# Pooling by banded products on TensorE, with 24 expert tiles transposed inside the pool mixer from GpSimd's queue

## The chip, the cores and the metric

One core of a Trainium2 chip runs the whole program in one launch. The metric is the device time in microseconds. TensorE (PE) multiplies, PEld is its weight load, VectorE is DVE, ScalarE is ACT, GpSimd is POOL, and SyncE (SP) issues the DMAs of the kernel before, all but its gathers.

## The reference

The input x is 512 tokens of 1024 features, in float32. Two blocks follow each other; the second one's first half and its expert half are given here in words.

```python
# block one, pool_mixer: windows w = 2, 4, 8, 16, a group of 512 channels each
u, z = split(x @ w_in)                              # 2048 columns each
m_g = (csum(u_g) - csum(u_g) lagged w) / min(t + 1, w) - u_g
m   = concat(m_g @ w_grp[g]) * scale
x   = layer_norm(ALPHA * x + (m * silu(z)) @ w_out)
# block two, first half
ada = silu(c) @ w_ada + b_ada                       # six vectors of 1024
# a conv branch and a gated linear recurrence (rg_lru), head norms, w_out
# block two, expert half (peer): top 16 of 128 x 128 experts for 8 heads,
# gelu(expert_u[idx] . h) * softmax(score), summed over expert_v[idx]
```

## The kernel before, in words

Every float32 product is made of three: an operand is split into a float32r part and its remainder (`split`, L108: the copy on ACT, the subtraction on DVE or, where asked, on POOL), and `mm3` (L138) multiplies high by high, high by low and low by high. Weights come through `wload` (L122), which splits them on the way; every `nload[1]`-th of them has its subtraction on POOL.

**The pool mixer** (the front) runs over the four groups. `x_group(g)` builds pooled tokens with the time axis along the free dimension: log2(w) shifted additions of `xT` on DVE, a scaled subtraction, a repair of the first w - 1 tokens, a split. `m_group` multiplies the group's `w_in` columns by that, so pooling comes ahead of the product. `gate_group` multiplies by `w_grp`, then scales by silu(z) (`z_group`); `y_group` multiplies by `w_out` and adds into `ya`. The last group goes through `last_group`, behind `p1.close()`, which gives the memory of the mixer's pools to those of the next stage (`wp2` among them, from which `last_group` takes its weights). In between, `ada(j)` sums 512 columns of `w_ada` on DVE from eight loads, and `ada_fin(j)` finishes them; its split has `pool=True`.

**The recurrence stage** (conv and lru branches) takes 20 products of 512 columns of the second `w_in`, each over eight slices of the features (`zchunk` and `zhalf`), with a chain of DVE and ACT work behind each (`lru`, `conv`, `headnorm`). Every weight's subtraction is on POOL here (`NZ = 1`). Between the products `pre_u` (L542) takes 20 tiles of `expert_u`, 128 rows each: four loads of half a tile into `praw`, one DVE transpose into `put`, one store to `ut_d`, and the same for the second half, all issued by SP, with two buffers of each kind.

**The expert half** finds the top keys, turns the scores into a dense weight matrix and runs over 128 tiles of experts. `stage_a(i)` takes a tile in one of three ways: for `i < NU` from `ut_d`, already transposed; for `NU <= i < RT = 38` by eight TensorE transposes; after that by a DVE transpose of its own load.

The program is traced in source order. A planner then orders each engine's instructions by its own cost model, with the source order as the priority, so that work of a later stage may stand early in a queue: polynomial work of L559 to L575 stands in the front on DVE, for one.

## Time and profile before

| | us |
|---|---|
| three runs, median (lowest to highest) | 1996.67 (1991.03 to 1996.69) |
| profiled execution, own time | 1993.15 |
| its span, first to last instruction | 1991.4 |
| PE busy in the span | 1800.5 |
| DVE busy in the span | 1783.6 |

The profiled execution's time is 1.75 us over its span. The front takes about 350 us of the span and the recurrence stage the next 200; the dense expert loop runs from about 1100 to the end. Busy shares are averages over stages with different limits, so a stage is read by its own window.

### The profile page before, as it was taken

How to read it: one execution, taken by the hardware profiler on the slowest of the kernel's cores; microseconds unless marked ns; L12 is line 12 of the kernel's file. 1: busy time of each engine (PE TensorE's matmuls, PEld its weight loads, DVE VectorE, ACT ScalarE, POOL GpSimd, SP SyncE). 2: the span in 40 equal slices, each digit the busy share in tenths (PEclk: the TensorE clock that was granted, in tenths of full speed). 3: DMA queues.
4: the chain of work that ended last, by engine and by line, in shares of the span. 5: the costliest groups of instructions: out<-in, count | busy, mean ns of one | idle time of the engine just before them, and what ended most of it. 6: DMA issues, size and time to landing. Idle time of an engine off the chain costs nothing.

```text
span 1991.4 us, 26565 instructions
## 1 busy us (share of the span) xinstructions
PE 1800.5 (90%) x9003; PEld 1568.3 (79%) x9003; DVE 1783.6 (90%) x3088; ACT 830.8 (42%) x1318; POOL 727.5 (37%) x492
## 2 busy tenths in 40 slices
PE   8999889896899978888887999998999998989997
PEld 6787677765689978888766898888888887878886
DVE  8989888889868999996897998999999999999956
ACT  4433333444553339988332332333232333332334
POOL 3113222333351000000133655556565556565514
PEclk9999999998899989999998999999999999999999
DMA  5554574465554233545959999999999999999922
GB/s 163 180 166 128 190 250 131 140 203 179 172 159 135 76 112 139 202 179 205 294 199 281 299 285 292 302 296 309 306 298 296 310 299 289 305 293 306 293 102 96
DMA packets 288293, 441.13 MB, mean 222 GB/s; under 512 B 24600, under 2 KB 203652, under 8 KB 285084
## 3 DMA queue, kind: packets, MB, share of 16 engines
q1 hardware_dynamic: 251292, 305.19, 51.1%
q0 software_dynamic: 36864, 134.23, 20.5%
q8 instruction: 71, 1.16, 0.2%
q14 instruction: 66, 0.54, 0.1%
HBM read 393.11 MB, written 46.23 MB: 221 GB/s over the span
## 4 chain that ended last, share of the span: by engine, by line
DVE 36%; DMA 24%; PE 17%; issue 12%; ACT 7%; SPq 2%; POOL 2%; DVEq 0%; POOLq 0%; ACTq 0%
DMA uraw<-in_expert_u 11%; DVE ut L540 5%; DMA gu<-in_expert_u,idx 3%; DMA gv<-in_expert_v,idx 3%; DMA araw<-in_w_ada 3%; PE bank L139 3%; PE bank L141 3%; PE bank L140 3%; ACT gs L1136 2%; DVE acc L1204 2%; DVE ul L117 2%; DVE wlo L117 2%; ACT o L1098 2%; DVE junk L1193 2%; DVE sw L240 2%
## 5 line engine op out<-in xcount | busy, mean ns | idle before, releaser
L115 POOL TENSOR_TENSOR wlo<-wraw,whi 128x1024 fp32r<-128x1024 f32 x111 | 292.3, 2635 | 782.4 <-ACT whi L113 766.8
L141 PE MATMUL aux<-h2h,ul 128*128 128x384 f32 x1024 | 360.7, 353 | 59.8 <-DVE ul L117 53.5
L139 PE MATMUL aux<-h2h,uh 128*128 128x384 f32 x1024 | 355.9, 348 | 4.9 <-ACT uh L884 1.8
L140 PE MATMUL aux<-h2l,uh 128*128 128x384 f32 x1024 | 353.6, 345 | 0.0
L113 ACT ACTIVATE whi<-wraw 128x1024 fp32r<-128x1024 f32 x218 | 228.3, 1051 | 196.4 <-DMA wraw<-in_expert_v 68.5
L140 PE MATMUL o<-wlo,wh 128*128 128x512 f32 x756 | 297.7, 394 | 13.8 <-DVE wlo L117 13.7
L141 PE MATMUL o<-whi,wl 128*128 128x512 f32 x756 | 296.6, 392 | 0.0
L139 PE MATMUL o<-whi,wh 128*128 128x512 f32 x756 | 290.1, 395 | 5.2 <-ACT whi L113 5.2
L141 PEld LDWEIGHTS aux<-h2h,ul 128*128 128x128 f32 x1024 | 198.6, 194 | 76.6 <-DVE ul L117 68.7
L1181 POOL DMA_INDIRECT gv<-in_expert_v,idx x128 | 186.8, 1460 | 186.0 <-DVE acc L1204 150.4
L1181 POOL DMA_INDIRECT gu<-in_expert_u,idx x128 | 167.5, 1309 | 161.3 <-DVE junk L1193 127.7
L139 PEld LDWEIGHTS aux<-h2h,uh 128*128 128x128 f32 x1024 | 198.6, 194 | 10.3 <-ACT gl L905 2.4
L113 ACT ACTIVATE uh<-ut 128x1024 fp32r<-128x1024 f32 x90 | 95.3, 1058 | 262.2 <-PE aux L140 174.5
L540 DVE STREAM_TRANSPOSE ut<-uraw 128x1024 f32<-128x1024 f32 x90 | 200.0, 2222 | 4.7 <-DMA uraw<-in_expert_u 4.7
L140 PEld LDWEIGHTS aux<-h2l,uh 128*128 128x128 f32 x1024 | 197.9, 193 | 3.7
L1193 DVE SCALAR_TENSOR_TENSOR junk<-gu,hrow 128x1024 bf16<-128x1024 f32 x128 | 168.3, 1315 | 19.8 <-DMA gu<-in_expert_u,idx 19.6
L1204 DVE SCALAR_TENSOR_TENSOR acc<-gv,cf,acc 128x1024 f32<-128x1024 f32 x127 | 169.6, 1335 | 17.6 <-DMA gv<-in_expert_v,idx 15.1
L140 PEld LDWEIGHTS o<-wlo,wh 128*128 128x128 f32 x756 | 143.3, 190 | 43.9 <-DVE wlo L117 16.5
L113 ACT ACTIVATE wh<-gl 128x384 fp32r<-128x384 f32 x128 | 66.7, 523 | 253.2 <-PE o L140 234.3
L139 PEld LDWEIGHTS o<-whi,wh 128*128 128x128 f32 x756 | 143.3, 190 | 33.0 <-ACT whi L113 6.1
L141 PEld LDWEIGHTS o<-whi,wl 128*128 128x128 f32 x756 | 143.3, 189 | 30.7
L117 DVE TENSOR_TENSOR wlo<-wraw,whi 128x1024 fp32r<-128x1024 f32 x107 | 150.6, 1409 | 7.2 <-ACT whi L113 7.2
(376 smaller groups left out, 3607.4 us busy)
## 6 DMA issues: line engine op xcount, KB each, us to landing
wraw<-in_expert_v SPq DMA_DIRECT2D x128, 512.0 KB
uraw<-in_expert_u SPq DMA_DIRECT2D x360, 128.0 KB
araw<-in_w_ada SPq DMA_DIRECT2D x96, 256.0 KB
g_d<-gs SPq DMA_DIRECT2D x24, 1024.0 KB
gt<-g_d SPq DMA_DIRECT2D x15, 1536.0 KB
wraw<-in_pool_w_in SPq DMA_DIRECT2D x32, 512.0 KB
wraw<-in_w_in SPq DMA_DIRECT2D x20, 512.0 KB
praw<-in_expert_u SPq DMA_DIRECT2D x160, 64.0 KB
```

Of the source, the lines that this page charges most:

```text
L113: S.activation(hi, src, AF.Copy)
L115: G.tensor_tensor(lo, src, hi.bitcast(F32), op=OP.subtract)
L117: V.tensor_tensor(lo, src, hi.bitcast(F32), op=OP.subtract)
L139: i = PE.matmul(out, lhsT=l[0], rhs=r[0], start=first, stop=False)
L140: PE.matmul(out, lhsT=l[0], rhs=r[1], start=False, stop=False)
L141: PE.matmul(out, lhsT=l[1], rhs=r[0], start=False, stop=last)
L240: V.tensor_tensor(nxt[:, :, step:], cur[:, :, step:], cur[:, :, :T - step], op=OP.add)
L540: V.transpose(out=ut.rearrange("p k (a r) -> p a k r", r=32), in_=raw.rearrange("p a (c k) -> p a k c", k=KD))
L1098: S.activation(o2[:, u], iorow, AF.Abs, bias=sT[:, 1, t0 + u:t0 + u + 1], scale=-1.0)
L1181: G.indirect_dma_start(out=r, out_offset=None, in_=src, in_offset=bass.IndirectOffsetOnAxis(ap=idx[t][:, s:s + 1], axis=0))
L1193: paced(V.scalar_tensor_tensor(junk, r, 1.0, hrow[t], op0=OP.mult, op1=OP.mult, accum_out=cf[t][:, s:s + 1]))
L1204: paced(V.scalar_tensor_tensor(acc[t], r, cf[t][:, s:s + 1], acc[t], op0=OP.mult, op1=OP.add))
```

## The change

- `u_group(g)` multiplies x (as the stationary operand) by the group's `w_in` columns: tokens on the partitions, 96 products of 512 columns as `m_group` had, in four banks at once, and four splits of 128x512.
- `pooled(g, u)` multiplies u by a banded matrix of w ones less w on the diagonal: for each of 4 x 4 blocks two products of 128 columns and one or two of 16 columns at the block's edge. The scale 1/w is folded into the copy from the bank.
- `bands()` builds the four band matrices and their first-tile forms once. `x_group`, `xT` and its four POOL additions go.
- No subtraction is left on POOL in the front or in the recurrence stage (`NZ`, `nload[1] = 3` removed, the `ada_fin` split on DVE).
- `pre_u` takes 24 tiles instead of 20. All are called inside the mixer's loop over groups 0 to 2, eight per group; its loads and stores are issued by POOL, and its `praw` and `put` buffers lie in the mixer's pool. The calls inside the recurrence find nothing left to do.
- The `ada_fin` calls stand after `gate_group` for groups 1 and 2 and after the loop for the last.

```diff
-AF_ = (1, 1, 0, 0)
-NZ = 1
+AF_ = (1, 1, 1)
+NZ = 1 << 30
-NU = 20
+NU = 24
+NP1 = 1
+BW = P + 16
...
-    sp_ = p1.enter_context(tc.tile_pool(name="sp_", bufs=3))
+    up = p1.enter_context(tc.tile_pool(name="up1", bufs=2))
-    xT = xp.tile([P, KD, T], F32, name="xT")
...
-    for q in range(4):
-        G.tensor_tensor(xT[:, 2 * q:2 * q + 2, :], xh[:, q].bitcast(F32), xl[:, q].bitcast(F32), op=OP.add)
...
+    def u_group(g):
+        bs = [bank() for _ in range(NT)]
+        for kk in range(4):
+            w = wload(w_in[kk * 256:(kk + 1) * 256, g * 512:(g + 1) * 512].rearrange("(k p) c -> p k c", p=P), 2)
+            for t in range(NT):
+                s = slice(t * P, (t + 1) * P)
+                for j in range(2):
+                    x = at(xhl, 2 * kk + j)
+                    mm3(bs[t], (x[0][:, s], x[1][:, s]), (w[0][:, j], w[1][:, j]), kk + j == 0, kk == 3 and j == 1)
+        uh = [act.tile([P, 2, T], F32R, name="ah", tag="ah") for _ in range(2)]
+        ul = [act.tile([P, 2, T], F32R, name="al", tag="al") for _ in range(2)]
+        for t in range(NT):
+            split(uh[t // 2][:, t % 2], ul[t // 2][:, t % 2], bs[t])
+        return uh, ul
+
+    def pooled(g, u):
         r = []
+        band, first, rest = band_[g]
         for c in range(4):
-            w = wcols(w_in, g * 512 + c * P, P)
             b = bank()
-            for k in range(KD):
-                mm3(b, (w[0][:, k], w[1][:, k]), at(xg, k), k == 0, k == KD - 1)
+            part = lambda t, i: u[i][t // 2][:, t % 2, c * P:(c + 1) * P]
+            for t in range(NT):
+                m = (band if t else first)[:, :P]
+                o = b[:, t * P:(t + 1) * P]
+                e = o[:, :16]
+                PE.matmul(o, lhsT=part(t, 0), rhs=m, start=True, stop=False)
+                if t == 0:
+                    PE.matmul(e, lhsT=part(t, 0), rhs=rest, start=False, stop=False)
+                else:
+                    PE.matmul(e, lhsT=part(t - 1, 0), rhs=band[:, P:], start=False, stop=False)
+                    PE.matmul(e, lhsT=part(t - 1, 1), rhs=band[:, P:], start=False, stop=False)
+                PE.matmul(o, lhsT=part(t, 1), rhs=m, start=False, stop=True)
...
-            split(h, l, b)
+            S.activation(h, b, AF.Copy, scale=1.0 / WINDOWS[g])
+            V.scalar_tensor_tensor(l, b, 1.0 / WINDOWS[g], h.bitcast(F32), op0=OP.mult, op1=OP.subtract)
...
-        split(hi, lo, acc, True)
+        split(hi, lo, acc)
...
+    def u_load(raw, i, a0, na, q_=nc.sync):
...
+                    u_load(raw, npre, 2 * h, 2, G)
...
+                    G.dma_start(ut_d[npre, :, h], ut.rearrange("p k e -> p (k e)"))
...
-    xg = act_tiles()
-    list(x_group(0, xg))
-    nload[1] = 3
     accs = {}
-    for g in range(4):
-        mhl = m_group(g, xg)
...
+    mhl = pooled(0, u)
+    for g in range(3):
+        pre_u(NP1)
+        u = u_group(g + 1)
+        pre_u(NP1)
+        pre_u(NP1)
         ghl = gate_group(g, mhl, sz)
         if AF_[g] == 1:
             ada_fins()
-        xg = act_tiles()
-        sz = z_group(g + 1, x_group(g + 1, xg))
+        sz = z_group(g + 1)
+        pre_u(NP1)
+        mhl = pooled(g + 1, u)
...
         for _ in y_group(g, ghl):
-            pass
+            pre_u(1)
+    ada_fins()
     p1.close()
```

## Rows read from the trace of the kernel before

**Rows 1.** The span by stage: busy time of each engine in each stretch (in brackets the instructions), the granted TensorE clock as a share of full speed, the mean busy share of the DMA engines, and GB/s.
```profile
0.00:45.00 45.00, 35.41 (x170) 30.48 (x171) 37.62 (x53) 19.53 (x29) 17.73 (x62) 0.98 0.58 176
45.00:200.00 155.00, 153.18 (x656) 122.34 (x655) 149.55 (x200) 60.04 (x98) 36.80 (x13) 0.99 0.50 155
200.00:350.00 150.00, 135.77 (x619) 108.17 (x618) 128.49 (x167) 48.67 (x73) 39.53 (x21) 0.99 0.59 188
350.00:550.00 200.00, 163.61 (x726) 127.38 (x726) 175.92 (x212) 100.59 (x153) 65.63 (x38) 0.91 0.56 172
550.00:620.00 70.00, 69.94 (x421) 64.16 (x420) 45.44 (x61) 35.80 (x61) 31.40 (x29) 1.00 0.55 173
```

**Rows 2.** What TensorE waited for, from 45 to 350 us: total, times, longest.
```profile
PE bank L140 <- DVE wlo L117: 5.2, 3, 2.9
PE bank L140 <- DVE sl L117: 2.7, 2, 2.2
```

**Rows 3.** What TensorE waited for longest from 350 to 550 us, and then what SP's queue waited for there.
```profile
PE aux L620 <- ACT sq L616: 27.4, 5, 9.1
...
SPq L552 <- DVE put L540: 42.9, 30, 4.6
SPq L124 <- POOL wlo L115: 28.5, 6, 15.6
```

**Rows 4.** TensorE's instructions in order of time (start, us, instruction, how many merged): products of 512 columns, of 256 columns, and of 128 columns, these in plain float32.
```profile
24.08 0.39 PE L139 MATMUL bank<-xh,whi 128*128 128x512 f32 x1
24.31 0.40 PE L140 MATMUL bank<-xl,whi 128*128 128x512 f32 x1
...
16.21 0.28 PE L141 MATMUL bank<-xh,wlo 128*128 128x256 f32 x1
16.33 0.28 PE L139 MATMUL bank<-xh,whi 128*128 128x256 f32 x1
...
799.78 2.84 PE L1135 MATMUL bank<-og,o 128*128 128x128 f32 x24
```

**Rows 5.** Groups of DVE instructions from 0 to 335 us: shapes, count, busy time and mean ns of one, idle time before them.
```profile
L240 DVE TENSOR_TENSOR sw<-xT 128x1022 f32<-128x1022 f32 x16 | 23.8, 1487 | 0.0
L240 DVE TENSOR_TENSOR sw<-sw 128x1020 f32<-128x1020 f32 x12 | 16.7, 1394 | 0.0
L240 DVE TENSOR_TENSOR sw<-sw 128x1016 f32<-128x1016 f32 x8 | 12.1, 1509 | 0.0
L240 DVE TENSOR_TENSOR sw<-sw 128x1008 f32<-128x1008 f32 x4 | 4.8, 1190 | 0.0
L244 DVE SCALAR_TENSOR_TENSOR xe<-sw,xT 128x1024 f32<-128x1024 f32 x16 | 23.6, 1477 | 0.2
L117 DVE TENSOR_TENSOR al<-xe,ah 128x1024 fp32r<-128x1024 f32 x16 | 22.7, 1423 | 0.4 <-ACT ah L113 0.4
L117 DVE TENSOR_TENSOR wlo<-wraw,whi 128x1024 fp32r<-128x1024 f32 x39 | 55.7, 1430 | 1.9 <-ACT whi L113 1.9
L117 DVE TENSOR_TENSOR sl<-bank,sh 128x512 fp32r<-128x512 f32 x16 | 10.8, 681 | 4.3 <-ACT sh L113 4.3
```

**Rows 6.** POOL's and DVE's instructions around 110 us in order of time, the POOL row first.
```profile
110.49 2.41 POOL L115 TENSOR_TENSOR wlo<-wraw,whi 128x1024 fp32r<-128x1024 f32 x1 [17.35 <-ACT whi L113]
...
107.94 1.21 DVE L240 TENSOR_TENSOR sw<-sw 128x1020 f32<-128x1020 f32 x1
110.80 3.18 DVE L240 TENSOR_TENSOR sw<-sw 128x1016 f32<-128x1016 f32 x1
```

**Rows 7.** Groups of POOL instructions from 0 to 335 us (the first two) and from 350 to 550 us (the third).
```profile
L115 POOL TENSOR_TENSOR wlo<-wraw,whi 128x1024 fp32r<-128x1024 f32 x17 | 49.2, 2894 | 169.4 <-ACT whi L113 169.4
L115 POOL TENSOR_TENSOR ahl<-acc,ahl 128x512 fp32r<-128x512 f32 x12 | 23.7, 1975 | 62.9 <-DVE acc L343 36.3 <-ACT ahl L113 14.2 <-DMA ada_d<-araw 9.1
...
L115 POOL TENSOR_TENSOR wlo<-wraw,whi 128x1024 fp32r<-128x1024 f32 x25 | 62.3, 2492 | 126.6 <-ACT whi L113 114.6 <-DMA praw<-in_expert_u 11.9
```

**Rows 8.** The transposes of the pre-turned tiles (group of DVE, 350 to 550 us), and SP's issues of their loads (ns min/median/max, first and last start).
```profile
L540 DVE STREAM_TRANSPOSE put<-praw 128x512 f32<-128x512 f32 x40 | 46.2, 1158 | 12.8 <-DMA praw<-in_expert_u 12.7
L535 SPq DMA_DIRECT2D praw<-in_expert_u x160: 354/425/1389, 365.0 to 521.8; - x160
```

**Rows 9.** The only DMAs that POOL issues in this kernel, gathers of 128 rows: groups from 1100 to 1900 us, and four in order of time (in brackets POOL's idle time before).
```profile
L1181 POOL DMA_INDIRECT gv<-in_expert_v,idx x128 | 186.8, 1460 | 186.0 <-DVE acc L1204 150.4 <-DMA uraw<-in_expert_u 12.4 <-issue 6.4
L1181 POOL DMA_INDIRECT gu<-in_expert_u,idx x119 | 157.7, 1325 | 139.9 <-DVE junk L1193 112.6 <-DMA uraw<-in_expert_u 9.2 <-issue 8.1
...
1226.63 1.28 POOL L1181 DMA_INDIRECT gu<-in_expert_u,idx  x1 [0.30 <-issue]
1228.22 0.94 POOL L1181 DMA_INDIRECT gv<-in_expert_v,idx  x1 [0.30 <-issue]
```

**Rows 10.** The first and last start of one line each: the first DVE work of `last_group`, the last addition of `y_group` (ns min/median/max).
```profile
L297 DVE SCALAR_TENSOR_TENSOR sz<-bank,cols,sz x8: 466/476/485, 324.1 to 344.6; 128x256 f32<-128x256 f32 x8
L329 DVE TENSOR_TENSOR ya<-ya,bank x16: 668/674/680, 188.4 to 302.8; 128x512 f32<-128x512 f32 x16
```

**Rows 11.** A tile's two ways in `stage_a`: subtraction from a bank after TensorE transposes (two per tile), and from `ut` (one per tile), then the TensorE transposes themselves.
```profile
L886 DVE TENSOR_TENSOR ul<-aux,uh x36: 630/680/692, 756.1 to 961.4; 128x512 fp32r<-128x512 f32 x36
L895 DVE TENSOR_TENSOR ul<-ut,uh x20: 1199/1214/1226, 587.7 to 724.2; 128x1024 fp32r<-128x1024 f32 x20
L882 PE MATMUL aux<-ident,uraw x144: 270/273/377, 742.5 to 953.7; 128*128 128x128 f32 x144
```

## What the change will do, predicted blind

> **What bounds the kernel now.** I first cut the span by stage [rows 1], since the page's 90% for both PE and DVE is an average. From 45 to 200 us PE is busy 153 of 155 us and DVE 150: the front is bound by PE, with DVE as full behind it. From 200 to 350 us PE falls to 136 of 150 and DVE to 128: neither is full, and the list of PE's waits [rows 2] names splits on DVE, weights' and banks'. From 350 to 550 us, the recurrence stage, PE is busy 164 of 200 at a granted clock of 0.91, while DVE has 176. PE's longest wait there [rows 3] is for the head norms' squares, the end of chains that alternate between DVE and ACT, so a late DVE is what PE pays for. SP's queue waits 42.9 us there for transposes and 28.5 us for subtractions on POOL, with the next weights' loads behind them. From 550 us PE is full again [rows 1], and what follows is not touched but for four tiles. So the change is worth what it gives in two windows: the front, where PE counts, and the recurrence, where DVE counts.
>
> **PE in the front.** `u_group` has the 96 products of 512 columns that `m_group` had, and `z_group`, `gate_group` and `y_group` stay. Two starts in a row stand 0.23 us apart for 512 columns and 0.12 us for 256 [rows 4]. `pooled` adds 60 products per group (3 for the first token tile and 4 for the others, times 4 blocks of channels), 240 in all, 128 of them with 128 columns and 112 with 16. No such product is in the trace. From above, none should cost more than a 256-column one: 240 x 0.12 = 29 us. From below, by columns alone, (0.23 - 0.12) / 256 = 0.00043 us each: 128 x 0.065 + 112 x 0.018 = 10 us. The nearest row in shape is the plain float32 product of 128 columns, 24 in 2.84 us or 0.118 each [rows 4]; but its operands are not float32r, and the float32r ones run faster for the same columns. I take 0.09: 240 x 0.09 = +22 us, all on PE's path where PE is full. The Trainium skill's page "TensorE: Matmul & The Clock Gate", section "Back-to-back issue gap", gives about 81 ns per product at 128 columns in a stream of weight loads and products; by it the sum here would be 19 us instead of 22, and no row here shows it.
>
> **DVE in the front.** Gone are the shifted additions, 23.8 + 16.7 + 12.1 + 4.8 = 57.4 us, the scaled subtractions, 23.6, and the splits of pooled tokens, 22.7 [rows 5]; with small repairs about 112 us. New are 16 splits of u at 0.68 us (11) [rows 5], 48 transposes at 1.158 us (56) [rows 8], the 17 subtractions that POOL had at 1.21 (21), 12 of `ada_fin` at some 0.68 (8) [rows 5 to 7], and some 40 small operations for the bands, at 0.2 us about 7. That is 103 us, so the work hardly changes: -9 us. What changes is the lock: an addition on DVE that takes 1.21 us took 3.18 us beside a POOL subtraction of 2.41 us [rows 6], and the mean of the weights' subtractions on DVE is 1.43 us, not 1.21 [rows 5]. So one product on POOL took up to 2.0 us from DVE, more than the 1.21 us it saved there. Without them the 39 weights' subtractions alone get back 39 x 0.22 = 9 us, and others perhaps as much again. DVE falls from 316 us of the first 350 to about 288.
>
> For PE I count from this: 3 us at the start (9.6 us idle in the first 45, part of it for pooled tokens that are not needed any more), and half of the 14 us idle from 200 to 350, 7 us; bounds 0 and 17. The front is then 22 - 3 - 7 = +12 us.
>
> **POOL's queue.** POOL now issues 24 x 10 = 240 DMAs, of which SP issued 200 at 0.43 us each [rows 8]. The only DMAs of POOL in the trace are gathers of 128 rows: 0.94 us at the least, 1.39 us in the mean of both groups, with 0.30 us to the next [rows 9]. A load here has 64 pieces of 1 KB and a store 128 of 2 KB. Bounds for one: 0.94 + 0.30 = 1.24 and 1.39 + 0.30 = 1.69 us, so 298 to 405 us for all, from about 3 us on, as nothing else is on POOL and the loads depend on nothing. I take the lower end, since most DMAs here describe half as many pieces: done at about 300 us. The cover is the front itself: the buffers lie in the mixer's pool, which `last_group`'s weights take over, and its first DVE work starts at 324 us [rows 10], at 336 with the 12 us above. That needs 1.35 us or less per DMA (with 12 us for the weights' way to that product, (336 - 12) / 240). If it is more, the weights of `last_group` wait, and DVE, in order, stands at transposes whose data is late; behind those are the subtractions that PE waits for.
>
> The DMA engines have room: they are busy 0.50 to 0.59 of the front at 155 to 188 GB/s [rows 1], and 25 MB more (24 tiles of 0.5 MB, in and out) are 72 GB/s over 350 us, which would bring them to some 0.75 to 0.8.
>
> **The recurrence stage.** DVE loses 40 transposes, 46.2 us [rows 8], and gains 25 subtractions at 1.21 us, 30 us, that were POOL's [rows 7]. The lock gives back at most 25 x 2.0 = 49 us [rows 6]; I take two thirds, 33, since a DVE operation with one operand in SBUF need not stop. So 176 - 46 + 30 - 33 = 127 us of the 200. A weight's remainder is also ready in 1.2 instead of 2.5 us [rows 7], and SP's queue has no transposes to wait for [rows 3]. PE's idle time there is 36 us, and the granted clock of 0.91 says that the engine, after its gaps, spent 18% of the window at 1.2 instead of 2.4 GHz. I take three quarters of the idle time, -27 us; the rest are the chains' own lengths on ACT. Bounds: -8 (the waits on POOL and on praw stay hidden behind the chains) and -45 (all of the idle time and a part of the clock).
>
> **Four tiles** go from TensorE transposes to a load from `ut_d`: DVE 2 x 0.68 against 1.21 us, PE 8 transposes less [rows 11]. That is under 5 us of PE in a stage in which it waits for ACT's work; I count 0.
>
> **The sum** is +22 - 3 - 7 - 27 = -15 us on the profiled execution's own 1993.15 us: 1978 us. This execution is 3.5 us below the median of the runs shown and within their spread. The ends of all bounds give +29 - 0 - 8 = +21 (2014) and +10 - 17 - 45 = -52 (1941).
>
> **The rivals.** *POOL paces the front (slower).* Each 0.1 us over 1.35 per DMA costs 24 us. From 1.35 + 15 / 240 = 1.41 us on, the change loses; at 1.50 it is 36 us, 2014 us, and at the gathers' mean 1.69 it would be 2059. For it: the gathers' mean; POOL's queue is in order, so a store that waits for its transpose holds the next loads. Against it: the gathers ran between products on POOL and with twice the pieces of a load, and two buffers let the loads of one half run ahead of the other's store. A rule of the skill speaks for it too: the page "SBUF — State Buffer", section "Who interferes with whom", has DVE's two-port modes (copy, tensor_scalar) shut GpSimd out of writing descriptors for the whole instruction. By it the DMAs of the front would lie nearer to 1.69 than to 1.24 us; the gathers' spread from 0.94 to 1.28 us and more [rows 9] does not tell what they waited for. On the bounds alone, with the middle of 1.24 and 1.69 at 1.47 and most DMAs half as large, the chance is 0.25.
>
> *No change.* The recurrence's chains are bound by their own lengths, as PE's wait for squares that come from ACT can be read, and PE gets back nothing in the front: +22 - 20 = +2, 1995 us. Chance 0.13.
>
> *More than forecast.* The small products cost by their columns, 10 us, the front gets back 10, and the recurrence stage all of its idle time, 36: 1957 us or less. Chance 0.14.
>
> *As forecast*, 1962 to 1989 us: 0.48.
>
> **Numbers.** A difference of 0.3%, 6 us, is about what these runs can tell from none. Faster by more: 0.48 + 0.14 = 0.62; within: 0.13; slower: 0.25. The range goes from 1943 (the low end of the bounds, but for 2 us) to 2020, which takes in the first rival up to 1.52 us per DMA; beyond stay about 0.15 above and 0.04 below. The forecast case alone is 1962 to 1989.
>
> **What would show it.** In the changed kernel's trace: starts of the small products about 0.09 us apart (10 to 29 us in all is right); no DVE operation of 1024 elements over 1.3 us before 550 us; POOL's DMAs under 1.35 us from start to start, the last store before 320 us, no wait of DVE for `praw` of more than 15 us in total; the front ending (first work of `last_group`) about 12 us later; the 200 us of the recurrence stage shortened by 20 or more with a granted clock above 0.91. The forecast is wrong if POOL issues until the end of the mixer and DVE or ACT stand behind it, or if the planner's order puts transposes ahead of splits that PE needs.

## The result: 0.55% slower, and the profile after

The changed kernel takes 2003.94 us (median of six runs, 2001.77 to 2005.77), the kernel before 1992.65 beside it (six runs, 1988.64 to 1996.69). The ratio is 1.0055, interval 1.0038 to 1.0071: slower by about 11 us where 15 us less was forecast. That is inside the range of 1943 to 2020 us that was given, but by luck: its upper end stood there for a slow POOL queue, and this is not what happened. The profiled execution has 2005.77 us, its span 2004.0.

The same windows as in [rows 1], of the changed kernel (busy time of each engine, granted clock, DMA share, GB/s):

```profile
0.00:45.00 45.00, 35.35 (x179) 31.12 (x180) 27.12 (x82) 17.29 (x23) 20.38 (x91) 1.00 0.85 250
45.00:200.00 155.00, 155.00 (x706) 129.46 (x705) 111.67 (x160) 48.42 (x65) 76.92 (x143) 0.94 0.74 225
200.00:350.00 150.00, 141.16 (x636) 114.54 (x634) 111.65 (x149) 36.06 (x49) 35.38 (x65) 0.94 0.73 225
350.00:550.00 200.00, 177.49 (x852) 143.57 (x851) 150.68 (x243) 109.64 (x168) 7.39 (x17) 0.92 0.31 93
550.00:620.00 70.00, 67.12 (x372) 58.83 (x371) 45.66 (x64) 32.48 (x56) 17.63 (x24) 0.98 0.51 157
```

DVE is relieved everywhere (149.55 to 111.67 us in the second window). PE is busy in all of the 155 us, and its granted clock there is 0.94 instead of 0.99: it is busier, and slower.

Fixed windows mix stages once the stages have moved, so I cut both kernels at two events: the first DVE work of `last_group`, which ends the front, and the first DVE work on the recurrence stage's output (`ot`), which ends that stage. The kernel before:

```profile
0.00:324.10 324.10, 300.87 (x1311) 241.25 (x1312) 292.94 (x372) 119.19 (x181) 83.40 (x88) 0.99 0.58 184
324.10:558.60 234.50, 195.70 (x895) 154.23 (x895) 203.74 (x261) 112.48 (x174) 82.57 (x48) 0.92 0.51 157
```

The changed kernel:

```profile
0.00:367.60 367.60, 338.06 (x1538) 279.10 (x1539) 257.16 (x403) 105.14 (x139) 132.68 (x298) 0.93 0.73 223
367.60:570.10 202.50, 190.76 (x914) 155.15 (x913) 157.15 (x247) 115.42 (x176) 7.39 (x17) 0.96 0.31 93
```

The front is 43.5 us longer, the recurrence 32.0 us shorter, and the rest is equal: 1432.8 us to the end of the span before, 1433.9 after. So the recurrence did what was forecast (-27), and the whole miss lies in the front, where +12 was forecast.

To split the front I set each of PE's start-to-start times against the median spacing of its shape at full clock; this is an estimate, and another grouping of the shapes moves some 3 us between the terms. Before: 287.7 us of products, 2.6 added by half clock, 29.5 of waits. After: 316.4, 17.4 and 29.1. So +28.7 us are products' own length, +14.8 the clock, and the waits hardly changed.

The new products in the changed kernel, in order of time (start, us, instruction): a block of 15 at full clock, then some of the same shapes a few us later.

```profile
62.48 0.28 PE L284 MATMUL bank<-first,ah 128*128 128x128 f32 x1
62.59 0.23 PE L286 MATMUL bank<-rest,ah 128*128 128x16 f32 x1
62.67 0.31 PE L290 MATMUL bank<-first,al 128*128 128x128 f32 x1
62.81 0.28 PE L284 MATMUL bank<-band,ah 128*128 128x128 f32 x1
62.93 0.23 PE L288 MATMUL bank<-band,ah 128*128 128x16 f32 x1
63.01 0.26 PE L289 MATMUL bank<-band,al 128*128 128x16 f32 x1
63.12 0.31 PE L290 MATMUL bank<-band,al 128*128 128x128 f32 x1
...
64.16 0.28 PE L284 MATMUL bank<-first,ah 128*128 128x128 f32 x1
...
67.52 0.41 PE L284 MATMUL bank<-band,ah 128*128 128x128 f32 x1
67.73 0.32 PE L288 MATMUL bank<-band,ah 128*128 128x16 f32 x1
67.91 0.36 PE L289 MATMUL bank<-band,al 128*128 128x16 f32 x1
68.12 0.45 PE L290 MATMUL bank<-band,al 128*128 128x128 f32 x1
```

A block takes 64.16 - 62.48 = 1.68 us, 0.112 per product, and 16 of them 26.9 us. A product of 16 columns (0.08 to 0.11) is hardly cheaper than one of 128 (0.11 to 0.14). The rows of the weight loads suggest why: each product has a load of its own, of 128 columns whatever the product's width, and in the burst these start 0.11 us apart.

```profile
62.53 0.19 PEld L286 LDWEIGHTS bank<-rest,ah 128*128 128x128 f32 x1
62.65 0.19 PEld L290 LDWEIGHTS bank<-first,al 128*128 128x128 f32 x1
62.76 0.19 PEld L284 LDWEIGHTS bank<-band,ah 128*128 128x128 f32 x1
```

At 67.5 us the same spacings are 0.21, 0.18, 0.21. The windows around the point where they change show the clock's two levels, 2.4 and then 1.2 GHz:

```profile
55.00:64.70 9.70, 9.70 (x63) 8.64 (x62) 5.03 (x10) 5.50 (x9) 4.04 (x8) 1.00 0.57 172
64.70:74.90 10.20, 10.20 (x39) 9.14 (x39) 8.74 (x20) 1.45 (x3) 3.21 (x6) 0.50 0.73 240
```

PE never idles here; what it did ahead of the fall was the burst of 60 small products from 60.8 us on. The clock falls inside each of the four bursts (at 64.7, 132.9, 221.7 and 317.3 us), and twice more in the front, at 249.0 behind a wait of 3.5 us and at 351.4 us in the waits at the front's end.

POOL's queue, forecast at 1.24 us or more per DMA (duration in ns, min/median/max; first and last start), and the transposes it feeds:

```profile
L402 POOL DMA_DIRECT2D praw<-in_expert_u x192: 533/533/800, 1.5 to 279.5; - x192
L419 POOL DMA_DIRECT2D ut_d<-put x48: 557/586/588, 20.9 to 285.9; - x48
```

And what DVE waited for these loads in the front (total, times, longest):

```profile
DVE put L407 <- DMA praw<-in_expert_u: 13.8, 11, 2.5
```

With stores done by 286 us and 13.8 us of waits in all, POOL is not what paces the front.

What answers [rows 10], the last addition of `y_group` and the first work of `last_group`:

```profile
L363 DVE TENSOR_TENSOR ya<-ya,bank x16: 679/681/683, 236.1 to 347.9; 128x512 f32<-128x512 f32 x16
L331 DVE SCALAR_TENSOR_TENSOR sz<-bank,cols,sz x8: 475/478/484, 367.6 to 393.0; 128x256 f32<-128x256 f32 x8
```

The last addition ends at 348.6 us, so there is a gap of 19 us in which PE has little but the closing products of the modulation vector (`ada_fin`). In the kernel before, 62 of the 96 products of `m_group(3)` lay in the 20.6 us there. I call this the seam.

### The profile page after: what moved, and what is told of

Read it like the earlier page. It is cut to its first block, busy times and chain, and to the rows that moved or that the text cites. A ratio compares the mean times of both kernels' runs of the same rounds, so it can differ in the third digit from the quotient of the medians.

```text
span 2004.0 us, 26936 instructions
## 1 busy us (share of the span) xinstructions
PE 1834.7 (92%) x9211; PEld 1610.4 (80%) x9211; DVE 1711.4 (85%) x3101; ACT 819.9 (41%) x1274; POOL 679.2 (34%) x669
## 4 chain that ended last, share of the span: by engine, by line
DVE 22%; DMA 17%; PE 13%; issue 9%; ACT 6%; POOL 2%; SPq 1%; DVEq 0%; POOLq 0%; ACTq 0%
DMA uraw<-in_expert_u 8%; DMA gv<-in_expert_v,idx 4%; DMA gu<-in_expert_u,idx 4%; DVE ut L407 4%; PE bank L1170 2%; DVE junk L1228 2%; DVE acc L1239 2%; ACT gs L1171 2%; PE aux L142 2%; ACT o L1133 2%; PE aux L140 2%; PE aux L141 2%; DVE ul L118 2%; PE o L141 1%; PE o L142 1%
## 5 line engine op out<-in xcount | busy, mean ns | idle before, releaser
L116 POOL TENSOR_TENSOR wlo<-wraw,whi 128x1024 fp32r<-128x1024 f32 x63 | 155.3, 2465 | 482.3 <-ACT whi L114 481.0
L141 PE MATMUL o<-wlo,wh 128*128 128x512 f32 x756 | 297.5, 394 | 14.9 <-DVE wlo L118 13.8
L118 DVE TENSOR_TENSOR wlo<-wraw,whi 128x1024 fp32r<-128x1024 f32 x155 | 201.7, 1303 | 71.2 <-ACT whi L114 68.7
L140 PEld LDWEIGHTS aux<-h2h,uh 128*128 128x128 f32 x1024 | 199.2, 195 | 13.9 <-ACT uh L919 6.8
L1228 DVE SCALAR_TENSOR_TENSOR junk<-gu,hrow 128x1024 bf16<-128x1024 f32 x128 | 178.9, 1398 | 14.0 <-DMA gu<-in_expert_u,idx 13.8
L1239 DVE SCALAR_TENSOR_TENSOR acc<-gv,cf,acc 128x1024 f32<-128x1024 f32 x127 | 176.3, 1388 | 8.6 <-DMA gv<-in_expert_v,idx 8.1
L114 ACT ACTIVATE wh<-gl 128x384 fp32r<-128x384 f32 x128 | 66.8, 522 | 244.3 <-PE o L141 235.9
```

The lines of the kernel that those rows point to most:

```text
L114: S.activation(hi, src, AF.Copy)
L116: G.tensor_tensor(lo, src, hi.bitcast(F32), op=OP.subtract)
L118: V.tensor_tensor(lo, src, hi.bitcast(F32), op=OP.subtract)
L140: i = PE.matmul(out, lhsT=l[0], rhs=r[0], start=first, stop=False)
L141: PE.matmul(out, lhsT=l[0], rhs=r[1], start=False, stop=False)
L1228: paced(V.scalar_tensor_tensor(junk, r, 1.0, hrow[t], op0=OP.mult, op1=OP.mult, accum_out=cf[t][:, s:s + 1]))
```

## The experiments

The times are medians; ratios are against the kernel before, run on the same chip. "Front" is the first work of `last_group`, "recurrence" the stretch from there to the first DVE work on its output, both of the profiled run. Numbers of theories in the expectations count anew by subject; each says what it means.

### Three parts that add up

**e6: the kernel before without GpSimd products in front and recurrence.**

```diff
-NZ = 1
+NZ = 1 << 30
-        split(hi, lo, acc, True)
+        split(hi, lo, acc)
-    nload[1] = 3
```

> The kernel before with its GpSimd products taken out of the front and put back to VectorE and nothing else: sums over windows, the order of the four U tiles and the transposes in the recurrence stay. What is computed is the same. Theory one (the lock between VectorE and GpSimd costs the kernel before something in its own front and in its own recurrence, and the recurrence's gain of the change comes mostly from the transposes that left it): VectorE gets some more to do in the front, its operations there lose their excess, the front ends within 5 us of the 324 us of before, and the recurrence still takes 225 to 240 us; time 1980 to 2005 us. Rival (most of the 32 us by which the change shortens the recurrence comes from the GpSimd products being gone): the recurrence falls to 205 to 215 us and the time to 1960 to 1975 us.

1988.78 us, ratio 0.9964 (0.9941 to 0.9987); front 311.9, recurrence 242.1.

**e5: the changed kernel without its moved transposes.** 20 tiles go back into the recurrence and to SP's queue; still no GpSimd products.

```diff
-NU = 24
+NU = 20
-                    u_load(raw, npre, 2 * h, 2, G)
+                    u_load(raw, npre, 2 * h, 2)
...
-            pre_u(1)
+            pass
```

> The tiles' transposes back in the recurrence stage: 20 tiles, loaded and stored by SP; bands and no GpSimd products as changed. If the front is bound by TensorE (its products, its clock), taking 48 transposes and 240 DMAs out of it leaves its end within 5 us of 367.6, and the recurrence stage gets 8 to 20 us longer: 2012 to 2024 us. If the transposes or the GpSimd queue stretch the front: its end 10 us earlier or more, and the time 2000 us or less.

2025.76 us, ratio 1.0199 (1.0136 to 1.0262); front 353.7, recurrence 241.5.

The windows of both stages of e6:

```profile
0.00:311.90 311.90, 296.55 (x1321) 240.05 (x1321) 275.54 (x392) 118.34 (x179) 14.54 (x61) 0.99 0.60 187
311.90:554.00 242.10, 201.03 (x889) 158.66 (x889) 203.14 (x301) 114.64 (x176) 7.48 (x17) 0.89 0.52 158
```

The recurrence of e5:

```profile
353.70:595.20 241.50, 200.56 (x914) 159.27 (x913) 198.97 (x287) 115.97 (x176) 4.89 (x17) 0.90 0.54 164
```

Before, e6, e5 and the changed kernel form a chain in which one part is added at a time:

| part | front | recurrence | ratio, from to |
|---|---|---|---|
| no GpSimd products (e6 - before) | -12.2 | +7.6 | 1 to 0.9964 |
| banded products, `ada_fin`'s new places (e5 - e6) | +41.8 | -0.6 | 0.9964 to 1.0199 |
| transposes moved (changed - e5) | +13.9 | -39.0 | 1.0199 to 1.0055 |
| sum | +43.5 | -32.0 | 1.0055 |

So the banded products are the loss: 42 us of front, for DVE work that PE hardly waited for. e6 and e5 differ there by 25.7 us of products, 15.4 of half clock and 0.8 of waits; the step holds the moved `ada_fin` too, which no run takes apart from it. The moved transposes are the gain, and cost 14 us in the front. Of e6's first theory the time held and the recurrence came out 2 us over its range; the front fell by more than it allowed, its waits from 29.5 to 19.0 us (4.2 of these at its very end, where PE stands idle). The rival, that most of the recurrence's gain comes from the missing GpSimd products, is refuted. e5 came out as neither of its theories says: its front ends 13.9 us before the changed kernel's, as its rival has it, but its recurrence is 39.0 us longer, not 8 to 20, and its time is over both ranges.

**e4: GpSimd products back in the changed kernel's recurrence.**

```diff
-NZ = 1 << 30
+NZ = 1
```

> The weights' subtractions of the recurrence stage and of w_out back on GpSimd (NZ = 1), all else as changed. If the lock and the late remainders were part of what the recurrence stage lost before: DVE operations of two SBUF operands there again take up to 2 us more, the stage from 367.6 to 570 us is 8 to 20 us longer, the time 2012 to 2024 us. If the moved transposes alone freed the stage: within 4 us of 2004.

2023.95 us, ratio 1.0181 (1.0128 to 1.0235). Its recurrence, which answers the changed kernel's 202.5 us above:

```profile
365.50:586.40 220.90, 194.44 (x897) 154.73 (x897) 172.43 (x216) 115.01 (x175) 81.62 (x46) 0.93 0.28 83
```

18.4 us more. DVE holds 172 us here against 157 although 30 subtractions of 1.21 us moved away from it: the lock of [rows 6] is real. The same 12 DVE operations in the changed kernel (368 to 570 us) and in e4 (366 to 586):

```profile
L647 DVE SCALAR_TENSOR_TENSOR xr<-zr,cols,xr 128x511 f32<-128x511 f32 (+2 forms) x12 | 8.9, 746 | 0.1
L647 DVE SCALAR_TENSOR_TENSOR xr<-zr,cols,xr 128x511 f32<-128x511 f32 (+2 forms) x12 | 19.1, 1592 | 0.4
```

But taking the GpSimd products out pays only together with the moved transposes. In the kernel before it made the recurrence 7.6 us longer (e6): DVE got 34 subtractions there, some 39 us, its other operations fell by about as much (the sum of their durations from 173 to 136 us), and it stayed as full as before.

### The products and the clock

**e1: the same 240 products, 15 behind each chunk of `z_group` instead of 60 in a row.**

```diff
-    def z_group(g):
+    def z_group(g, other=()):
...
             S.activation(r[c], b, AF.Silu)
+            next(other)
```

> Same work as the changed kernel; the small products of one block of 128 channels (15 of them) now follow each 512-column chunk of z_group, in place of 60 in a row. Theory one (the bursts of small products make the granted clock fall, and the 512-column products behind them run at half speed): the half-clock time in the front falls from some 50 us to under 20, the first work of last_group comes 10 to 15 us earlier than 367.6 us, and the time falls from 2004 to 1989 to 1994 us. Theory two (only the products' own length counts, the clock falls for other reasons): front and time within 4 us of the changed kernel.

1992.05 us, ratio 0.9987 (0.9959 to 1.0015); front 360.0. The second window of the front:

```profile
45.00:200.00 155.00, 155.00 (x753) 129.34 (x751) 114.48 (x165) 51.43 (x69) 78.65 (x145) 1.00 0.76 233
```

753 products instead of 706 in the same busy 155 us, at clock 1.00. The half clock's extra in the front falls from 17.4 to 5.6 us. In e1 the clock falls only right behind waits of PE of 2 us or more (at 235.9, 287.1 and 341.7 us), and no more while PE is busy. So the bursts are a cause of the fall. What it is worth is less than theory one says: PE's time at half clock in the front falls from 50 to 28 us, not to under 20, the waits grow by 5.6 us, and the front ends 7.6 us earlier, not 10 to 15. The recurrence is 2.7 us longer, so the rest of the 0.7% in time comes from behind both stages (see "A version that beats both").

**e8: e1 with 9 products per block instead of 15.** A product covers its own 128 columns and the next tile's 16; the first runs over 512 columns with zeros behind the band.

```diff
-                m = (band if t else first)[:, :P]
-                o = b[:, t * P:(t + 1) * P]
...
+                n = BW if t < NT - 1 else P
+                m = (band if t else first)[:, :n]
+                o = b[:, t * P:t * P + n]
```

> The changed kernel with the small products spread as in e1 and made fewer: each row tile's product runs over 144 columns, its own 128 and the first 16 of the next tile, so that 9 products stand for 15 in each block (144 instead of 240); the first of a block runs over all 512 columns with zeros behind the band. The result is the same sum. Theory one (the 28.7 us of these products is a cost per product, 0.08 to 0.14 us each, nearly independent of columns): 144 products take 15 to 20 us, the last group's first work comes 8 to 13 us earlier than e1's 360.0 us, time 1980 to 1988 us. Rival (the front is by now set by transfers and by the chain of the modulation vector, so that a shorter PE time there turns into waits): last group's first work within 4 us of e1's, time 1989 to 1996 us.

```profile
64.59 0.40 PE L286 MATMUL bank<-first,ah 128*128 128x512 f32 x1
64.83 0.17 PE L287 MATMUL bank<-rest,ah 128*128 128x16 f32 x1
64.85 0.31 PE L290 MATMUL bank<-first,al 128*128 128x144 f32 x1
65.00 0.28 PE L289 MATMUL bank<-band,ah 128*128 128x144 f32 x1
...
65.56 0.28 PE L290 MATMUL bank<-band,al 128*128 128x128 f32 x1
65.67 0.29 PE L437 MATMUL bank<-ident,vin 128*128 128x128 f32 x1
```

A block takes 1.08 us instead of 1.68, as the cost per product says (0.11 us for most with 144 columns too). The product of 16 columns takes 0.02 us here, where the one ahead of it runs over 512 columns and its own weight load starts with that one, at 64.59 us. The last y addition comes 12.4 us before e1's, the seam grows from 17.8 to 22.9 us, and the front ends at 352.7 us, 7.3 us before e1's and just short of the 8 to 13 of theory one. Yet the time is 1990.19 us, ratio 0.9978 (0.9948 to 1.0008): no gain over e1 that these runs can tell.

### The seam

**e2: the sums of the modulation vector ahead of `z_group`.**

```diff
+        for j in range(4 * g, 4 * g + 4):
+            accs[j] = ada(j)
         sz = z_group(g + 1)
...
-        for j in range(4 * g, 4 * g + 4):
-            accs[j] = ada(j)
```

> The four ada sums of each group stand ahead of z_group in place of behind pooled; nothing else is changed. Theory (the 19 us between the last addition of y_group at 348.6 and the first work of last_group at 367.6 us wait for the ada_fin chain that is left over at the end of the mixer): that stretch falls to 8 us or less, the time by 8 to 13 us, to 1991 to 1996 us. Rival (the stretch waits for last_group's weights, whose buffers are late): the stretch stays over 15 us and the time within 3 us.

2005.56 us, ratio 1.0064 (1.003 to 1.0099): nothing, the gap is 18.1 us, as the rival has it, though its reason is not tested here. The last of the third group's loads for these sums is issued at 339 us, at 341 in the changed kernel: by the code their accumulators come free only with the closings of the blocks ahead, which did not move.

**e7: e1, and the sums laid between the front's stages**, each group's closings behind its y products.

```diff
+        if g:
+            early(g, (0,))
         u = u_group(g + 1)
+        if g:
+            early(g, (1,))
...
+            early(g, (2, 3))
```

> The changed kernel with the small products spread as in e1, and the sums for the modulation vector of the second and third group laid between the front's stages (one block ahead of the u products, one behind them, two behind the gate) with each group's closing products behind that group's y products. Theory two (what stands between the third group's last y addition and the first product of the last group, 18 us in e1, is the chain of the last four blocks of that vector and the weights queued behind their loads on SyncE's queue): the gap falls to 3 to 8 us, the last group's first work is 8 to 15 us earlier than e1's 360.0 us, and the time is 1978 to 1986 us. Rival (the gap is set by the memory in which the last group's weights are loaded, which comes free only when the last z products have read x, and by the bandwidth of the transfers): the gap stays at 15 us or more, time 1988 to 1996 us, or later if the blocks' loads delay the weights of a stage.

1977.29 us, ratio 0.9914 (0.9879 to 0.9949), front 350.1. The time falls as expected, but not where it was expected: the gap stays at 16.6 us (333.5 to 350.1), and what fell is the way to the last y addition (342.2 us in e1), with waits 34.7 to 26.8 us and half clock's extra 5.6 to 2.7 us. The rival has the gap right and the time wrong.

**e10: the last group's weights issued ahead of the reads of the finished vector** (`last_group` yields once behind its loads), **and the last closings' DMAs on GpSimd's queue.** **e13: e10 with these reads on GpSimd's queue too.** The last three pairs of the diff are e13's.

```diff
-    ada_fins()
+    ada_fins(G)
...
     y_last = last_group(3, mhl, sz)
+    next(y_last)
...
-    nc.sync.dma_start(vin2[:24, :], ada_d[:3 * D].rearrange("(r c) -> r c", c=P))
+    G.dma_start(vin2[:24, :], ada_d[:3 * D].rearrange("(r c) -> r c", c=P))
...
-    nc.sync.dma_start(acol[:, 24:40].rearrange("p (j k) -> p j k", j=2),
+    G.dma_start(acol[:, 24:40].rearrange("p (j k) -> p j k", j=2),
...
-    bcast_row(g1r, ada_d[2 * D:3 * D])
+    bcast_row(g1r, ada_d[2 * D:3 * D], G)
```

> The changed kernel with two edits at the seam alone: the last group's weights are loaded before the reads of the finished modulation vector instead of behind them, and the closing pieces of that vector's last four blocks go over GpSimd's queue instead of SyncE's. Arithmetic unchanged. Theory three (in the changed kernel the 19 us between the third group's last y addition at 348.6 us and the first work of the last group at 367.6 us are an in-order queue: SyncE issues the weights at 358.9 us, behind the vector's write-backs and read-backs, which wait for VectorE): the weights are issued at 335 to 345 us, the gap falls to 3 to 9 us, the recurrence stays at 200 to 206 us, and the time is 1988 to 1996 us. Rival (the place of the weights in memory comes free late, or the weights' path over ScalarE stays behind the same sums): gap 14 us or more, 2000 to 2006 us.

> e10 with one thing more: the four reads that follow the finished modulation vector (its 24 rows, its columns, its first gate row, and the small norm row beside them) go over GpSimd's queue as well, so that nothing that waits for the vector stands on SyncE's queue ahead of the last group's weights. The order of all other instructions on every engine stays, but for one small VectorE operation. Theory three, sharpened (the gap of 15 us that e10 still has between the third group's last y addition at 349.4 us and the last group's first work at 364.5 us is SyncE's queue held by the read of the vector's columns, which waited 12.6 us for the write-backs and let the weights go only at 354.1 us): the weights are issued at 341 to 346 us, the gap falls to 3 to 9 us, the first work comes at 353 to 359 us, and the time is 1982 to 1989 us. Rival (TensorE is anyway held by the closing products of the vector and the split of the weights, which go through the same VectorE queue): gap 12 us or more, time 1989 to 1996 us.

e10: 1992.56 us, ratio 0.9998 (0.9981 to 1.0014), in theory three's range, but with the rival's gap, 15.2; its front is 3.1 us shorter and its recurrence 4.3 longer than the changed kernel's, so what it gains in time lies behind both. e13: 2000.71, ratio 1.0026 (1.0004 to 1.0049), outside both its ranges, gap 18.1, front 369.1. SP's queue in the changed kernel (start, us, instruction):

```profile
353.44 0.39 SPq L541 DMA_DIRECT2D acol<-ada_d  x1
354.92 2.17 SPq L389 DMA_DIRECT2D ada_d<-araw  x2
358.01 0.36 SPq L539 DMA_DIRECT2D n<-in_norm_g  x1
358.42 0.38 SPq L537 DMA_DIRECT2D vin<-ada_d  x1
358.85 0.95 SPq L125 DMA_DIRECT2D wraw<-in_pool_w_grp  x2
```

And in e13:

```profile
342.08 1.02 SPq L125 DMA_DIRECT2D wraw<-in_pool_w_grp  x2
```

The weights go 17 us earlier in e13, and the last group starts no earlier. So theory three, that SP's queue holds the seam, falls, but for the 3 us of e10. ACT in e13 shows what else does (start, us; in brackets the idle time and its end):

```profile
350.54 0.63 ACT L114 ACTIVATE ahl<-acc 128x512 fp32r<-128x512 f32 x1 [5.97 <-PE aux L387]
352.68 0.63 ACT L114 ACTIVATE ahl<-acc 128x512 fp32r<-128x512 f32 x1 [1.51 <-PE aux L388]
354.32 0.63 ACT L114 ACTIVATE ahl<-acc 128x512 fp32r<-128x512 f32 x1 [1.01 <-DVE ahl L118]
354.86 1.99 ACT L114 ACTIVATE whi<-wraw 128x1024 fp32r<-128x1024 f32 x2
```

The closings run in series, some 2 us each: copy on ACT, subtraction on DVE, two products on PE, addition on DVE, write. They share four buffers, stand behind the last y products on PE, and the weights' splits stand behind them on ACT and DVE.

**e15: the changed kernel without the closing of the last four blocks.**

```diff
+        if j >= 4:
+            nc.sync.dma_start(ada_d[(j + 4) * 512:(j + 5) * 512].rearrange("(o d) -> o d", o=1), r[0:1, :])
...
-    ada_fins()
     p1.close()
```

> The changed kernel without the closing of the modulation vector's last four blocks: their loads and their sums on VectorE stay, but their two products each, the splits on ScalarE, the addition and the write are left out; the rows of blocks 4 to 7 are written twice instead, so those of 8 to 11 hold other values. Theory four (what holds the last group is the closing itself, a chain of about 2 us a block that runs through ScalarE, TensorE and VectorE in turn behind the last y products, with the write-back and the read-back behind it, so that taking one queue out, as e10 and e13 did, moves nothing): the weights go by 346 us, the gap between the last y addition and the last group's first work falls from 19 us to 3 to 8 us, and the time is 1988 to 1995 us. Rival (the gap is the load and split of the last group's weights, whose memory comes free late): gap 14 us or more, 2000 to 2006 us.

```profile
L363 DVE TENSOR_TENSOR ya<-ya,bank x16: 628/680/683, 235.7 to 349.4; 128x512 f32<-128x512 f32 x16
L331 DVE SCALAR_TENSOR_TENSOR sz<-bank,cols,sz x8: 467/480/484, 357.0 to 383.5; 128x256 f32<-128x256 f32 x8
```

The gap is 6.9 us instead of 19.0 (the last addition ends at 350.1), the front's waits 20.7 instead of 29.1; 1996.21 us, ratio 1.0011 (0.9981 to 1.0041), 1 us over theory four's range. Theory four holds: the closing chain, with its writes and the reads that wait for them, is the seam, 12 us of it.

**e16: e11 (below), each of the last blocks closed behind one of the first four y products**, and one more block summed ahead of the gate.

```diff
-        for _ in y_group(g, ghl):
-            pre_u(1)
-        ada_fins(G)
+        for n, t in y_group(g, ghl):
+            if n:
+                pre_u(1)
+            elif g == 2:
+                ada_fin(8 + t, accs.pop(8 + t), G)
+        ada_fins()
```

> e11 with the whole vector and a better place for its last closings: three of the last four blocks are summed ahead of the third group's gate instead of two, the fourth behind it, and each block is closed behind one of the first four of the third group's eight y products instead of behind all of them. Theory four: the write-backs and the reads are done before the last y addition, the gap of 13.4 us in e11 falls to 3 to 7 us, first work at 334 to 340 us, and the time is 1957 to 1966 us. Rival (the weights' memory): gap 12 us or more, 1966 to 1974 us; or the earlier loads of the blocks delay the gate's weights, and what the seam gives is lost there.

1980.86 us, ratio 0.9936 (0.9908 to 0.9965). The gap is 5.0 us, as theory four says; but the last y addition comes at 340.0 us instead of 331.2, and the front ends at 345.0 us against 344.6. What the seam gave was lost ahead of it, as the last rival says: the third group's gate came at 280 us instead of 274. As the fronts are equal, the 12.7 us by which e16 takes longer than e11 are not the seam's: 3.8 are in the recurrence, the rest behind it.

### A version that beats both

These join edits whose diffs stand above: **e9** is e7 with e8's products; **e11** is e7 with e10's edits, but that the closings of all three groups go over GpSimd's queue; **e12** is e9 with the same; **e14** is e11 with e13's reads.

> The edits of e7 and e8 together. If both theories hold, their gains add, as PE sets the front: last group's first work 338 to 346 us, time 1968 to 1978 us, 0.8 to 1.2% under the kernel before. If only the products count: 1980 to 1988 us. If only the chain of the vector counts: 1978 to 1986 us. If the transfers set the front: 1988 to 1998 us.

> e7 (products spread, sums of the modulation vector between the front's stages) with the two seam edits of e10. Theory three: the gap of 16.6 us that e7 still has between the last y addition (333.5 us) and the last group's first work (350.1 us) falls to 2 to 7 us, first work at 336 to 342 us, time 1962 to 1972 us. Rival (the gap is the memory's): 1974 to 1982 us.

> e9 (e7 with 144 wide products instead of 240) with the two seam edits. Theory three: gap of 16.4 us falls to 2 to 7 us, first work at 330 to 336 us; time 1958 to 1974 us. As e9 came out no faster than e7 (1983.8 against 1977.3 us) although its front is 5.8 us shorter, the later stages decide the order between e11 and e12: if what the wide products save is kept, e12 is 3 to 8 us under e11; if it is given back behind 750 us, the two are equal within 3 us.

> e11 with the same four reads on GpSimd's queue. In e11 the read of the columns waited 10.5 us and the weights went at 335.9 us, 4.7 us behind the last y addition at 331.2 us; the first work came at 344.6 us. Theory three, sharpened: weights issued at 318 to 326 us, first work at 332 to 339 us, time 1956 to 1966 us. Rival (VectorE's queue holds TensorE as before): first work at 342 us or later, time 1965 to 1972 us.

| | front | recurrence | us | ratio |
|---|---|---|---|---|
| e9 | 344.3 | 206.9 | 1983.83 | 0.9951 (0.9928 to 0.9973) |
| e11 | 344.6 | 202.9 | 1968.20 | 0.9860 (0.9833 to 0.9886) |
| e12 | 338.3 | 207.6 | 1989.54 | 0.9971 (0.9948 to 0.9995) |
| e14 | 347.3 | 203.5 | 1975.22 | 0.9903 (0.9879 to 0.9928) |

By the ratios e11 is 1.4% under the kernel before and 1.9% under the changed one. Its profiled execution, the slowest of its six (1983.77 us, the others 1961.27 to 1973.23), by stages:

```profile
0.00:344.60 344.60, 324.31 (x1538) 267.60 (x1539) 255.83 (x403) 105.27 (x139) 144.49 (x322) 0.98 0.77 238
344.60:547.50 202.90, 190.10 (x914) 154.34 (x913) 158.12 (x247) 114.78 (x176) 5.19 (x17) 0.96 0.31 92
```

It has the same products as the changed kernel in a front 23 us shorter, at clock 0.98 instead of 0.93. Of the theories in e11's expectation, theory three has its time (1962 to 1972) but not its gap, which is 13.4 us; that the closing chain holds the seam was not known yet. e14's first work comes at 347.3 us, as its rival says (342 or later), and its time is 3 us over the rival's range. The wide products of e9 and e12 shorten the front by another 6 us, and the time is 6.5 and 21 us longer. e9's front is in the range for gains that add (338 to 346), its time is not; e12's gap is 13.4 us, not 2 to 7.

What comes behind the recurrence differs, although no edit is there: the planner wrote the later stages' queues in another order. On POOL, fourteen of the versions have one of two orders, which differ, for one, in whether six or seven subtractions of weights stand ahead of its work on `fgr`. The rest is an estimate: the median, less the front and the recurrence of the profiled execution and the 1.8 us or so outside the span.

| POOL's order behind the recurrence | versions | rest, us |
|---|---|---|
| as in the changed kernel | changed, e2, e6, e8, e9, e12, e15, e16 | 1427 to 1442 |
| the other | e1, e7, e10, e11, e13, e14 | 1419 to 1425 |

The two groups do not overlap, and their means are 11 us apart. This fits what the fronts leave unexplained: what e1 and e10 gain over the changed kernel beyond their fronts, e8 no faster than e1, e9 behind e7, e12 and e16 behind e11. So of the 36 us by which e11 is under the changed kernel, 23 are its front's and about 13 lie behind the recurrence. That the order is the cause is not shown: no run changes it alone, and the other engines' queues differ as well.

## Why the prediction was wrong, step by step

- **Small products, +22.** Inside its bounds, at their upper end: 26.9 us, 0.112 each instead of 0.09, and the front's products as a whole +28.7. Between the two ends I went below the row nearest in shape (0.118, [rows 4]) on the hope that float32r is faster; that row was right. Both bounds counted columns, and no row of the weight loads was looked at, which start 0.11 us apart. The Trainium skill's "TensorE: Matmul & The Clock Gate", section "Back-to-back issue gap", gives 81 ns; the trace, which decides here, shows 0.11 to 0.14 for 128 columns, and 0.08 only behind 16.
- **The clock, not in the sum.** This is the step that failed most: I priced the products at full clock only. 14.8 us of half clock came into the front, most of it in and behind their bursts (e1 takes 11.8 of it back by order alone, of which 5.6 return as waits). In the kernel before, the front ran at 0.99 [rows 1], and nothing in my argument asked whether another mix of products would keep it.
- **PE's recovery in the front, -10 (3 and 7).** It came to 0.4 us. The GpSimd products' leaving gave 10.5 us of waits (e6, as much as I counted); the moved transposes took 9.3 (waits 19.8 us in e5, 29.1 in the changed kernel), and the rest of the change 0.8. What I left out is that the moved work would bring waits of its own. Without the last four closings 8.4 of the 29.1 us are gone (e15), which overlaps with these. I had moved `ada_fin` in the text of the change and not asked what it would meet at the front's end, where `m_group(3)`'s products had covered it.
- **DVE in the front.** Forecast 316 to 288 in the first 350 us; it fell to 250 (27.12 + 111.67 + 111.65). No DVE operation of 1024 elements took over 1.3 us before 550 us, as forecast. The lock had cost more than the 18 us or so that I counted: in e6, with the same work, the sum of the durations of DVE's operations in the front, without the subtractions of weights and of `ada_fin`, is 224 us instead of 261. A relief of the engine that was full *behind* PE bought little.
- **POOL's queue, 1.24 to 1.69 us per DMA.** Measured 0.533 and 0.586, outside both bounds: a gather's duration does not bound a plain DMA's. The rival "POOL paces the front" is refuted. The slower end came, but by another mechanism. By the rule of "SBUF — State Buffer", section "Who interferes with whom", in the Trainium skill, DVE's two-port modes shut POOL out of writing descriptors while they run, which would stretch these DMAs. The trace agrees where it can show it: of DVE's larger operations in the front only the 12 `tensor_scalar` of `ada` are of that kind, two of them fell on a DMA, and these two DMAs are the only ones over 0.6 us but for the first, 0.65 and 0.77 us. What I got wrong is how often it would strike. The longer one, with the DVE operation beside it:

```profile
242.11 0.77 POOL L402 DMA_DIRECT2D praw<-in_expert_u  x1
242.29 0.49 DVE L375 TENSOR_SCALAR acc<-araw,cact 128x512 f32<-128x512 f32 x1 [0.96 <-DMA araw<-in_w_ada]
```

- **The recurrence, -27.** Right: -32.0. DVE fell from 203.74 to 157.15 us, 47 less where 49 was worked out; the clock rose from 0.92 to 0.96. PE's wait for head norms, 27.4 us in [rows 3], is gone from the list. The lock's part of DVE's work, put at 33 us, is about 37 by e6. The length of the stage follows DVE's work only in sum: without GpSimd's products alone it did not fall (e6, +7.6), and with them back it is 18.4 us longer (e4).
- **Four tiles, 0.** The rest behind the recurrence differs by 1 us in the two profiled executions. Between the versions it differs by up to 20, so this shows no more than that nothing large came of them.

The sum of the misses in the front: 28.7 - 22 = 6.7, 14.8, and 10 - 0.4 = 9.6, together 31 us, which is 43.5 - 12.

## What to carry to other kernels

When work is turned into many small products, price them by the number of products, look at the rows of their weight loads, and ask what the granted clock does in and behind a burst; spreading the same products between large ones took 7.6 us off the front here. Before relieving an engine, check that the one that sets the end waits for it in *that* stage: the 42 us went to relieve DVE in a front that PE bounds, the gain came from a stage in which PE waited for DVE. And when a block of products is reordered, look for the chain that it used to cover: queues in order hide it until the cover is gone, and moving one queue's share of such a chain gave 3 us of 19 (e10) or none (e13). Before a small gain in time is put down to an edit, look at whether the stages that the edit does not touch kept their order and their length.

## What the runs showed of the hardware

- In a run of small float32r products, starts stand 0.08 to 0.11 us apart behind 16 columns and 0.11 to 0.15 behind 128 or 144, against 0.12 for 256 and 0.23 for 512 [rows 4]; their weight loads start 0.11 us apart. Behind a product of 512 columns one of 16 took 0.02 us (e8). So up to 256 columns the width hardly counts here, and the rows suggest that the weight load is what is paid.
- The granted clock fell from 2.4 to 1.2 GHz while PE was busy without a gap, in each of four bursts of 60 small products; 15 at a time between 512-column products left it at 1.00 (45 to 200 us in e1).
- A plain DMA issued by POOL takes POOL 0.53 us (64 pieces of 1 KB) or 0.59 us (128 of 2 KB), also while DVE works beside it; 0.65 and 0.77 us where a DVE `tensor_scalar` of 512 elements ran beside it.
- The lock between DVE and POOL stretches DVE's operations by about 37 us in the recurrence of the kernel before (e6). POOL's products back in the changed kernel's recurrence, the lock and the later remainders together, make it 18 us longer (e4). Taking them away helps only where DVE has room: it lengthened the stage by 7.6 us when that was full of transposes (e6).
